# A layer norm inside a convolution module: from tokens on partitions to channels on partitions

## The chip, the cores and the metric

The kernel runs on one core of one Trainium2 chip. The time is device microseconds of one execution. A second source is the profile: one execution recorded instruction by instruction, with its own span, from the first to the last instruction. All positions in microseconds below are counted from the start of that span.

The core has five engines that work side by side, each through its own queue in program order: TensorE (in the profile PE for matrix products and PEld for the loading of their stationary operand), VectorE (DVE), ScalarE (ACT), GpSimd (POOL) and SyncE (SP), which here issues the loads from memory. They wait for each other through semaphores. Operands lie in SBUF, 128 partitions wide; TensorE writes its results into PSUM, and VectorE and ScalarE read and write both.

## The reference

A trunk of two layers over 256 tokens with 2048 channels. Layer 0 mixes tokens with a convolution module, layer 1 with latent attention, and a squared-ReLU MLP follows each. The change lies wholly in the convolution module:

```python
def layer_norm(x, g, b):
    xf = x.astype(jnp.float32)
    mu = jnp.mean(xf, axis=-1, keepdims=True)
    xc = xf - mu
    var = jnp.mean(xc * xc, axis=-1, keepdims=True)
    y = xc * lax.rsqrt(var + LN_EPS) * g.astype(jnp.float32) + b.astype(jnp.float32)
    return y.astype(x.dtype)

def conv_module(h, w_pw1, b_pw1, w_dw, b_dw, ln_g, ln_b, w_pw2, b_pw2):
    u = h @ w_pw1 + b_pw1
    a, gate = jnp.split(u, 2, axis=-1)
    u = a * jax.nn.sigmoid(gate)
    u = lax.conv_general_dilated(
        u, w_dw[:, None, :].astype(u.dtype), window_strides=(1,),
        padding=[(CONV_WIDTH - 1, 0)],
        dimension_numbers=("NWC", "WIO", "NWC"),
        feature_group_count=D_MODEL) + b_dw
    u = jax.nn.silu(layer_norm(u, ln_g, ln_b))
    return u @ w_pw2 + b_pw2
```

The mean and the variance of a token run over all its 2048 channels, so the norm cannot begin before the depthwise convolution of the last channels is done; gain and bias belong to a channel.

## The kernel before

**Data.** The 256 tokens are two blocks of 128 (T = 2), the 2048 channels sixteen chunks of 128 (KC = 16). Every full-precision product is made of three products of fp32r parts: an operand is split into a rounded high part and the rest, and high×high, low×high and high×low are added up in PSUM (`mm3`, L184 to L186). ScalarE makes the high part by a copy (`hi`, L158) and VectorE the rest by a subtraction (`lo`, L159); a unit of weights is split in two halves, by `conv_half`. Weights come through three buffers `raw`, one load of 1 MB to a unit, issued by SyncE; the halves lie in six buffers `hi` and six `lo`. So a load waits until both halves of the unit three before it are split, and a split waits until TensorE is done with the halves three units before.

**The convolution loop** (L712) runs over the chunks c. For each it makes the first pointwise product of the chunk (`conv_mm`), the gated value, and the 31 taps of the depthwise convolution, most of them on VectorE (`dve_tap`, L591). Here channels lie on partitions. The result of a chunk is written to `ca`, a pair of chunks to a tile, two such tiles in turn. Three chunks later TensorE turns it (`to_tokens`, L629), so that tokens lie on partitions and a pair of chunks fills one PSUM tile `ct`; VectorE takes the statistics of the pair from there (`bn_stats`, L639), and ScalarE copies the pair to `cn` (L641), in which all 2048 channels of a token end up on its partition.

**Between the loop and the second product.** TensorE makes transposes of the identity whose result nobody reads (`keep_warm`, counts in `N_WARM_LN`) so as not to stand idle. VectorE joins the statistics (`bn_aggr`, L755), and the function `rsqrt` makes the scale of each token out of the variance, with one square root on ScalarE (L207) and a Newton step on VectorE (L208 to L212). Mean and scale are one number to a token, that is one number to a partition of `cn`.

**The second product** (loop over m, L798) takes two chunks of channels and one 1 MB unit of weights (`NU + m`) to a step, 24 matmuls of 128x512 in all: two chunks by two column blocks by two token blocks by three. Its left operand has channels on partitions again. So `ln_norm` takes mean and scale from `cn` (L766, one VectorE instruction for two chunks of one token block, both factors as scalars of the partition), and `ln_swish` turns the pair back on TensorE (L776, four transposes into a tile `tr`, of which there are two), applies the sigmoid-weighted unit with gain and bias as scalars of the partition (L781, ScalarE), and splits the result into `sh` (L787, ScalarE) and `sl_` (L788, VectorE). The pairs 0 and 1 are done ahead of the loop; in step m stand `ln_norm(m+3)` and `ln_swish(m+2)` ahead of the products, then, in step 0, the second half of weight unit `NU+1`, after its first chunk; then the split of unit `NU+m+2`, the load of unit `NU+m+5`, and one addition of the output bias `b2` to the residual `xs` (L817). After the loop the four sums are added to `xs`, and `product_A` makes the other half of the columns.

Of the kernel before, what the change touches and what calls it, by code (L numbers as in the profile page):

```python
# [18 lines left out]
P = 128  # L19
# [30 lines left out]
LAST_REST = (20, 17, 0)  # L50
FILL_AT = (5, 15)
N_WARM = 14
N_WARM_LN = (8, 26, 14)
EPS = 1e-6
LN_EPS = 1e-5
SCALE = (DN + DR) ** -0.5
# [20 lines left out]
def trunk_kernel(  # L77
# [35 lines left out]
    def repool(name, **banks):  # L113

        psum_cx[0].close()
        psum_cx[0] = ExitStack()
        for kind, n in banks.items():
            psum[kind] = psum_cx[0].enter_context(tc.tile_pool(name=kind + name, bufs=n, space=PSUM, reuse_waits="tile"))
# [13 lines left out]
    def nm(s):  # L132
        uid[0] += 1
        return f"{s}_{uid[0]}"
# [5 lines left out]
    def tr_tile():  # L140
        return psum["tr"].tile([P, NB], F32, tag="tr", name=nm("tr"))
# [295 lines left out]
    with ExitStack() as cx:  # L437
# [10 lines left out]
        xn = cv.tile([P, T, D], F32, tag="tok", name="xn")  # L448
        b2 = cv.tile([P, D], F32, name="b2")

        cn = cv.tile([P, T, D], F32, tag="tok", name="cn")
        sh = cv.tile([P, KC, S], F32R, name="sh")
        sl_ = cv.tile([P, KC, S], F32R, name="sl_")
        stats = cv.tile([P, T, KC // 2, 6], F32, name="stats")
# [35 lines left out]
                    nc.tensor.matmul(o, wh[:, bs], xl(k), start=False, stop=False)  # L490
                    nc.tensor.matmul(o, wl[:, bs], xh(k), start=False, stop=k == KC - 1)  # L491

        pss, ubs, pcs, cas, cts, sides, left = {}, {}, {}, {}, {}, {}, {}
        rest = lambda c: LAST_REST[c - KC + 3] if c > KC - 4 else REST[min(c, 2)]
        n_side = lambda c: LAST_SIDE[c - KC + 3] if c > KC - 4 else SIDE
        tap = lambda c, w: w_dw[:, w * KC + c : w * KC + c + 1]

        def sum_tile():
            return psum["sum"].tile([P, NB], F32, tag="sum", name=nm("sum"))

        def ca_part(c):
            if c // 2 not in cas:
                cas[c // 2] = cv2.tile([P, 2 * S], F32, tag="ca", name=nm("ca"))
            return cas[c // 2][:, c % 2 * S : (c % 2 + 1) * S]

        def glu(c):
            ub = ubs[c] = cv2.tile([P, PAD + S], F32, tag="ub", name=nm("ub"), bufs=3)
# [62 lines left out]
        def dve_tap(c):  # L570
            w = left[c].pop(0)
            out = pcs[c]
            if w is None:
                nc.vector.tensor_tensor(out, out, sides[c][0], op=ALU.add)
                return
            if c == KC - 1 and w == LAST_PE + n_side(c):
                nc.vector.tensor_scalar(
                    out, ubs[c][:, w : w + S], scalar1=tap(c, w), scalar2=b_dw[:, c : c + 1],
                    op0=ALU.mult, op1=ALU.add,
                )  # L580
                return
            if not left[c]:
                if c == KC - 1:
                    half = cv2.tile([P, S], F32, tag="half", name=nm("half"), bufs=1)
                    nc.vector.scalar_tensor_tensor(
                        out=half, in0=ubs[c][:, w : w + S], scalar=tap(c, w), in1=out, op0=ALU.mult, op1=ALU.add
                    )
                    nc.vector.tensor_tensor(ca_part(c), last_sum[0], half, op=ALU.add)
                    return
                out = ca_part(c)  # L590
            nc.vector.scalar_tensor_tensor(  # L591
                out=out, in0=ubs[c][:, w : w + S], scalar=tap(c, w), in1=pcs[c], op0=ALU.mult, op1=ALU.add
            )
# [28 lines left out]
        def to_tokens(c):  # L622

            if c % 2 == 0:
                cts[c // 2] = acc_tile() if c == KC - 2 else tr_tile()
            ct = cts[c // 2]
            for t in range(T):
                q = 2 * t + c % 2
                nc.tensor.transpose(  # L629
                    ct[:, q * P : (q + 1) * P], ca_part(c)[:, t * P : (t + 1) * P], ident  # L630
                )

        def ln_stats(c):
            fill = []
            if c % 2 == 1:
                ct = cts[c // 2]
                for t in range(T):
                    fill.append(
                        lambda t=t: nc.vector.bn_stats(stats[:, t, c // 2, :], ct[:, t * S : (t + 1) * S])  # L639
                    )  # L640
                fill.append(lambda: nc.scalar.activation(  # L641
                    cn[:, :, (c - 1) * P : (c + 1) * P], ct.rearrange("p (t n) -> p t n", t=T), AF.Copy
                ))
            return fill

        conv_load(0)
        conv_load(1)
# [8 lines left out]
        with tc.manual_schedule():  # L656
# [55 lines left out]
            for c in range(1, KC + 1):  # L712
                n = UC * c
                conv_load(n + 3)
                glu(c - 1)
                fill = ln_stats(c - 4 if c < KC else KC - 3) if c > 3 else []
                fill, copies = fill[:T], fill[T:]
                if c < KC:
                    pss[c] = [acc_tile() for _ in range(2)]
                conv_half(n + (c < KC), 0)  # L720
                start_sum(c - 1)
                if c < KC:
                    conv_half(n + 1, 1)
                    dve_taps(c - 1, fill)
                    conv_load(n + 4)
                    side_sum(c - 1)
                    conv_mm(c, 0, 8)
                    if c < KC - 1:
                        conv_half(n + 2, 0)
                        conv_half(n + 2, 1)  # L730
                else:
                    side_sum(c - 1)
                    conv_half(n, 1)
                    conv_half(n + 1, 0)
                    dve_taps(c - 1, fill)
                    conv_load(n + 4)
                for f in copies:
                    f()
                if c < KC:
                    conv_mm(c, 8)  # L740
                    if c > KC - 4:
                        dgs.extend(diag(KC - 1, w) for w in range(len(dgs), min(len(dgs) + 8, LAST_PE)))
                    if c > 2:
                        to_tokens(c - 3)
                    conv_mm(c, 12)
# [7 lines left out]
            mv = small.tile([P, T, 2], F32, tag="mv", name=nm("mv"))  # L753
            for t in range(T):
                nc.vector.bn_aggr(mv[:, t, :], stats[:, t, :, :].rearrange("p a b -> p (a b)"))  # L755
            rl = rsqrt(mv[:, :, 1], T, LN_EPS, "n")
            warm(AF.Silu)
            repool("m", acc=6, tr=2)
            ps2 = [[acc_tile() for _ in range(T)] for _ in range(2)]

            def ln_norm(jj):
                ks = slice(2 * jj * P, (2 * jj + 2) * P)
                for t in range(T):
                    nc.vector.tensor_scalar(  # L766
                        cn[:, t, ks], cn[:, t, ks], scalar1=mv[:, t, 0:1], scalar2=rl[:, t : t + 1],
                        op0=ALU.subtract, op1=ALU.mult,
                    )

            def ln_swish(jj):
                pt = tr_tile()
                for j in range(2):
                    k = 2 * jj + j
                    for t in range(T):
                        nc.tensor.transpose(  # L776
                            pt[:, j * S + t * P : j * S + (t + 1) * P], cn[:, t, k * P : (k + 1) * P], ident
                        )
                for j in range(2):
                    k = 2 * jj + j  # L780
                    nc.scalar.activation(  # L781
                        pt[:, j * S : (j + 1) * S], pt[:, j * S : (j + 1) * S], AF.Silu,
                        bias=ln_b[:, k : k + 1], scale=ln_g[:, k : k + 1],
                    )
                sp = pt.rearrange("p (j n) -> p j n", j=2)
                ks = slice(2 * jj, 2 * jj + 2)
                nc.scalar.activation(sh[:, ks, :], sp, AF.Copy)  # L787
                nc.vector.tensor_tensor(sl_[:, ks, :], sp, sh[:, ks, :].bitcast(F32), op=ALU.subtract)  # L788

            sh_kt = lambda k, t: sh[:, k, t * P : (t + 1) * P]  # L790
            sl_kt = lambda k, t: sl_[:, k, t * P : (t + 1) * P]
            NP = KC // 2
            for jj in range(3):
                ln_norm(jj)
            for jj in range(2):
                ln_swish(jj)
            keep_warm(ident, N_WARM_LN[2])
            for m in range(NP):  # L798
                if m + 3 < NP:
                    ln_norm(m + 3)  # L800
                if m + 2 < NP:
                    ln_swish(m + 2)
                for j in range(2):
                    k = 2 * m + j
                    wh, wl = conv_w(NU + m, j)
                    for b in range(2):
                        bs = slice(b * NB, (b + 1) * NB)
                        for t in range(T):
                            mm3(ps2[b][t], sh_kt(k, t), sl_kt(k, t), wh[:, bs], wl[:, bs], k == 0, k == KC - 1)
                    if m == 0 and j == 0:  # L810
                        conv_half(NU + 1, 1)
                conv_split(NU + m + 2)
                conv_load(NU + m + 5)

                t, i = divmod(m, NNB)
                sl = slice(i * NB, (i + 1) * NB)
                nc.vector.tensor_tensor(xs[:, t, sl], xs[:, t, sl], b2[:, sl], op=ALU.add)  # L817

        ssq, add, prepare = residual_stage(True, g_mlp[0])
        for b in range(2):  # L820
# [590 lines left out]
```

## Time and profile before

| what | us |
|---|---|
| median of three executions | 2000.11 |
| lowest and highest of them | 1999.77 and 2000.18 |
| the profiled execution, its own time | 1998.02 |
| span of that execution, first to last instruction | 1996.2 |
| convolution loop and taps, by position | about 32 to 217 |
| norm until the first of the second products | 217 to 224.2 |
| second product, first half of its columns | 224.2 to 270.2 |

Lines of three views are quoted below. A line of the timeline gives start, duration, engine, line of the kernel, operation, output and inputs, shape, and how many instructions were merged into it; in square brackets stand the idle time before it and what ended that. Merged instructions overlap, so the duration of a line of several is less than the sum of its parts. A line of the groups gives line, engine, operation, shapes and count, then the busy time in us and the mean duration of one in ns, then the idle time before them. A line of the windows gives, for one stretch, the busy time of PE, PEld, DVE, ACT and POOL with the number of instructions, then the granted TensorE clock (1.00 is full), the share of the DMA engines and GB/s.

### The profile page before, as it was taken

How to read it: one execution, taken by the hardware profiler on the slowest of the kernel's cores; microseconds unless marked ns; L12 is line 12 of the kernel's file. 1: busy time of each engine (PE TensorE's matmuls, PEld its weight loads, DVE VectorE, ACT ScalarE, POOL GpSimd, SP SyncE). 2: the span in 40 equal slices, each digit the busy share in tenths (PEclk: the TensorE clock that was granted, in tenths of full speed). 3: DMA queues.
4: the chain of work that ended last, by engine and by line, in shares of the span. 5: the costliest groups of instructions: out<-in, count | busy, mean ns of one | idle time of the engine just before them, and what ended most of it. 6: DMA issues, size and time to landing. Idle time of an engine off the chain costs nothing.

```text
span 1996.2 us, 27870 instructions
## 1 busy us (share of the span) xinstructions
PE 1971.5 (99%) x11060; PEld 1727.9 (87%) x11060; DVE 1214.7 (61%) x1805; ACT 975.7 (49%) x1385; POOL 224.0 (11%) x184
## 2 busy tenths in 40 slices
PE   7999999999999999999999999999999999999998
PEld 7999788888888888888899998888888888888886
DVE  6999867556544555655556665656654545665553
ACT  5456655445333444544456665545443334454443
POOL 5999200000000000000001310000000000000000
PEclk9999999999999999999999999999999999999999
DMA  7666365665555666555555445666655566665653
GB/s 239 185 183 183 130 198 182 190 190 189 195 198 195 190 190 190 190 190 190 190 159 176 120 147 181 200 190 190 190 190 190 195 194 189 191 191 195 194 190 105
DMA packets 243265, 367.57 MB, mean 184 GB/s; under 512 B 15416, under 2 KB 89792, under 8 KB 242880
## 3 DMA queue, kind: packets, MB, share of 16 engines
q1 hardware_dynamic: 242400, 364.68, 57.6%
q8 instruction: 86, 1.41, 0.3%
q10 hardware_dynamic: 736, 1.12, 0.2%
q14 instruction: 43, 0.35, 0.0%
HBM read 363.68 MB, written 2.10 MB: 183 GB/s over the span
## 4 chain that ended last, share of the span: by engine, by line
PE 90%; DVE 8%; ACT 1%; DMA 0%; issue 0%; POOL 0%; SPq 0%; ACTq 0%; DVEq 0%
PE acc L403 23%; PE acc L186 16%; PE acc L184 16%; PE acc L185 16%; PE acc L404 12%; DVE sum L591 6%; PE acc L490 1%; PE acc L489 1%; PE acc L491 1%; PE tr L241 1%; PE sum L539 0%; DMA xs<-in_x 0%; PE acc L1185 0%; ACT hi L158 0%; PE acc L1049 0%
## 5 line engine op out<-in xcount | busy, mean ns | idle before, releaser
L159 DVE TENSOR_TENSOR lo<-raw,hi 128x1024 fp32r<-128x1024 f32 (+2 forms) x630 | 760.9, 1211 | 693.4 <-ACT hi L158 681.6
L158 ACT ACTIVATE hi<-raw 128x1024 fp32r<-128x1024 f32 (+1 forms) x696 | 723.2, 1046 | 787.8 <-PE acc L185 452.2
L403 PE MATMUL acc<-xt,hi 128*128 128x512 f32 x2048 | 710.6, 390 | 0.0
L404 PE MATMUL acc<-xt,lo 128*128 128x256 f32 x2048 | 577.7, 282 | 0.0
L403 PEld LDWEIGHTS acc<-xt,hi 128*128 128x128 f32 x2048 | 384.5, 188 | 80.5
L184 PE MATMUL acc<-hi,gh 128*128 128x512 f32 x1024 | 398.6, 389 | 0.0
L186 PE MATMUL acc<-lo,gh 128*128 128x512 f32 x1024 | 398.4, 389 | 0.0
L185 PE MATMUL acc<-hi,gl 128*128 128x512 f32 x1024 | 398.4, 389 | 0.0
L404 PEld LDWEIGHTS acc<-xt,lo 128*128 128x128 f32 x2048 | 387.1, 189 | 0.1
L185 PEld LDWEIGHTS acc<-hi,gl 128*128 128x128 f32 x1024 | 192.2, 188 | 39.8
L184 PEld LDWEIGHTS acc<-hi,gh 128*128 128x128 f32 x1024 | 192.2, 188 | 39.8
L186 PEld LDWEIGHTS acc<-lo,gh 128*128 128x128 f32 x1024 | 192.2, 188 | 39.8
L591 DVE SCALAR_TENSOR_TENSOR sum<-ub,w_dw,sum 128x256 f32<-128x256 f32 x400 | 162.9, 484 | 7.5 <-ACT sum L547 6.4
L159 POOL TENSOR_TENSOR lo<-raw,hi 128x1024 fp32r<-128x1024 f32 x66 | 157.7, 2413 | 21.7 <-ACT hi L158 21.7
L489 PE MATMUL acc<-xt,hi 128*128 128x256 f32 x512 | 144.4, 282 | 0.0
L490 PE MATMUL acc<-xt,hi 128*128 128x256 f32 x512 | 143.1, 279 | 0.9 <-DVE xt L197 0.9
L491 PE MATMUL acc<-xt,lo 128*128 128x256 f32 x512 | 143.1, 279 | 0.3 <-POOL lo L159 0.3
L490 PEld LDWEIGHTS acc<-xt,hi 128*128 128x128 f32 x512 | 96.3, 188 | 1.1 <-DVE xt L197 1.1
L491 PEld LDWEIGHTS acc<-xt,lo 128*128 128x128 f32 x512 | 96.2, 188 | 0.6 <-POOL lo L159 0.6
L489 PEld LDWEIGHTS acc<-xt,hi 128*128 128x128 f32 x512 | 96.3, 188 | 0.0
L980 POOL MEMSET pad_kv<- 128x8 f32 x1 | 0.1, 105 | 770.1 <-PE acc L186 770.1
L411 ACT ACTIVATE v<-acc 128x256 f32<-128x256 f32 x128 | 46.4, 381 | 25.4 <-PE acc L404 25.4
(240 smaller groups left out, 1785.0 us busy)
## 6 DMA issues: line engine op xcount, KB each, us to landing
raw<-in_mlp_w SPq DMA_DIRECT2D x256, 1024.0 KB, 5.1
raw<-in_conv_w_pw SPq DMA_DIRECT2D x64, 512.0 KB, 5.2
raw<-in_conv_w_pw SPq DMA_DIRECT2D x16, 1024.0 KB, 5.0
raw<-in_mla_w_o SPq DMA_DIRECT2D x16, 1024.0 KB, 5.5
raw<-in_mla_w_kv_up SPq DMA_DIRECT2D x8, 1024.0 KB, 5.5
raw<-in_mla_w_in SPq DMA_DIRECT2D x8, 576.0 KB, 3.7
raw<-in_mla_w_in SPq DMA_DIRECT2D x4, 1024.0 KB, 6.1
raw<-in_mla_w_q_up SPq DMA_DIRECT2D x16, 256.0 KB, 3.8
```

Of the source, the lines that this page charges most:

```text
L158: nc.scalar.activation(hi, raw[:, js, :], AF.Copy)
L159: eng.tensor_tensor(lo, raw[:, js, :], hi.bitcast(F32), op=ALU.subtract)
L184: nc.tensor.matmul(ps, sh, mh, start=start, stop=False)
L185: nc.tensor.matmul(ps, sl, mh, start=False, stop=False)
L186: nc.tensor.matmul(ps, sh, ml, start=False, stop=stop)
L403: nc.tensor.matmul(ps[b], wh[:, bs], xhl(k), start=k == 0, stop=False)
L404: nc.tensor.matmul(ps[b][:, :S], wl[:, bs], xh(k), start=False, stop=k == KC - 1)
L411: nc.scalar.activation(v[:, b, :], o[:, S:], AF.Copy)
L489: nc.tensor.matmul(o, wh[:, bs], xh(k), start=k == 0, stop=False)
L490: nc.tensor.matmul(o, wh[:, bs], xl(k), start=False, stop=False)
L491: nc.tensor.matmul(o, wl[:, bs], xh(k), start=False, stop=k == KC - 1)
L591: nc.vector.scalar_tensor_tensor(out=out, in0=ubs[c][:, w : w + S], scalar=tap(c, w), in1=pcs[c], op0=ALU.mult, op1=ALU.add)
```

## The change

The norm is done where the convolution leaves its result, with channels on partitions. The sixteen chunks are kept in one tile `ca`, which takes the place of `cn`; the copies to `cn` fall away. The transposes of `to_tokens` stay, for the statistics alone. Mean and scale now differ along the row and not along the partitions, so each is spread by two transposes of a column read 128 times over: every partition of the PSUM tiles `mean` and `scale` then holds the 256 values of all tokens. Norming is two VectorE instructions (subtract the row, multiply by the row) in place of one with two scalars; the four transposes of each pair in `ln_swish` fall away, and ScalarE and VectorE work in place on `ca` in SBUF. The first two chunks are done one by one. The additions of `b2` move from all steps to the last three. The counts of idle transposes change.

```diff
-N_WARM_LN = (8, 26, 14)
+N_WARM_LN = (8, 17, 6, 10)
...
-        cn = cv.tile([P, T, D], F32, tag="tok", name="cn")
+        ca = cv.tile([P, KC, S], F32, tag="tok", name="ca")
...
-            fill = []
-            if c % 2 == 1:
-                ct = cts[c // 2]
-                for t in range(T):
-                    fill.append(
-                        lambda t=t: nc.vector.bn_stats(stats[:, t, c // 2, :], ct[:, t * S : (t + 1) * S])
-                    )
-                fill.append(lambda: nc.scalar.activation(
-                    cn[:, :, (c - 1) * P : (c + 1) * P], ct.rearrange("p (t n) -> p t n", t=T), AF.Copy
-                ))
-            return fill
+            if c % 2 == 0:
+                return []
+            ct = cts[c // 2]
+            return [
+                lambda t=t: nc.vector.bn_stats(stats[:, t, c // 2, :], ct[:, t * S : (t + 1) * S])
+                for t in range(T)
+            ]
...
+            repool("m", acc=6, tr=2)
+
+            mean, scale = (tr_tile()[:, :S] for _ in range(2))
+
+            def spread(dst, src):
+                for t in range(T):
+                    nc.tensor.transpose(dst[:, t * P : (t + 1) * P], src(t).broadcast_to([P, P]), ident)
+
+            spread(mean, lambda t: mv[:, t, 0:1])
             rl = rsqrt(mv[:, :, 1], T, LN_EPS, "n")
             warm(AF.Silu)
-            repool("m", acc=6, tr=2)
+            keep_warm(ident, N_WARM_LN[2])
+            spread(scale, lambda t: rl[:, t : t + 1])
             ps2 = [[acc_tile() for _ in range(T)] for _ in range(2)]
...
-            def ln_norm(jj):
-                ks = slice(2 * jj * P, (2 * jj + 2) * P)
-                for t in range(T):
-                    nc.vector.tensor_scalar(
-                        cn[:, t, ks], cn[:, t, ks], scalar1=mv[:, t, 0:1], scalar2=rl[:, t : t + 1],
-                        op0=ALU.subtract, op1=ALU.mult,
+            def ln_op(k, n, row, op):
+                o = ca[:, k : k + n, :]
+                row = row.rearrange("p (a n) -> p a n", a=1).broadcast_to([P, n, S])
+                nc.vector.tensor_tensor(o, o, row, op=op)
+
+            def ln_norm(k, n=2):
+                ln_op(k, n, mean, ALU.subtract)
+                ln_op(k, n, scale, ALU.mult)
+
+            def ln_swish(k, n=2):
+                for j in range(k, k + n):
+                    nc.scalar.activation(
+                        ca[:, j, :], ca[:, j, :], AF.Silu, bias=ln_b[:, j : j + 1], scale=ln_g[:, j : j + 1]
                     )
...
+                nc.scalar.activation(sh[:, k : k + n, :], ca[:, k : k + n, :], AF.Copy)
+                nc.vector.tensor_tensor(
+                    sl_[:, k : k + n, :], ca[:, k : k + n, :], sh[:, k : k + n, :].bitcast(F32), op=ALU.subtract
+                )
...
-            for jj in range(3):
-                ln_norm(jj)
-            for jj in range(2):
-                ln_swish(jj)
-            keep_warm(ident, N_WARM_LN[2])
+
+            for row, op in ((mean, ALU.subtract), (scale, ALU.mult)):
+                for k in range(2):
+                    ln_op(k, 1, row, op)
+            for k in range(2):
+                ln_swish(k, 1)
+            ln_norm(2)
+            ln_swish(2)
+            ln_norm(4)
+            keep_warm(ident, N_WARM_LN[3])
             for m in range(NP):
                 if m + 3 < NP:
-                    ln_norm(m + 3)
+                    ln_norm(2 * (m + 3))
                 if m + 2 < NP:
-                    ln_swish(m + 2)
+                    ln_swish(2 * (m + 2))
...
-                t, i = divmod(m, NNB)
-                sl = slice(i * NB, (i + 1) * NB)
-                nc.vector.tensor_tensor(xs[:, t, sl], xs[:, t, sl], b2[:, sl], op=ALU.add)
+                for q in {NP - 3: (0, 1, 4), NP - 2: (5, 2, 3), NP - 1: (6, 7)}.get(m, ()):
+                    t, i = divmod(q, NNB)
+                    sl = slice(i * NB, (i + 1) * NB)
+                    nc.vector.tensor_tensor(xs[:, t, sl], xs[:, t, sl], b2[:, sl], op=ALU.add)
```

More of the change, by code (lines that the diff above doesn't have):

```diff
@@ L491, in conv_mm @@
                     nc.tensor.matmul(o, wl[:, bs], xh(k), start=False, stop=k == KC - 1)
-        pss, ubs, pcs, cas, cts, sides, left = {}, {}, {}, {}, {}, {}, {}
+        pss, ubs, pcs, cts, sides, left = {}, {}, {}, {}, {}, {}
         rest = lambda c: LAST_REST[c - KC + 3] if c > KC - 4 else REST[min(c, 2)]
@@ L499, in sum_tile @@
             return psum["sum"].tile([P, NB], F32, tag="sum", name=nm("sum"))
[L501 to L504, printed above, removed]
         def glu(c):
@@ L587, in dve_tap @@
                     )
-                    nc.vector.tensor_tensor(ca_part(c), last_sum[0], half, op=ALU.add)
+                    nc.vector.tensor_tensor(ca[:, c, :], last_sum[0], half, op=ALU.add)
                     return
-                out = ca_part(c)
+                out = ca[:, c, :]
             nc.vector.scalar_tensor_tensor(
@@ L629, in to_tokens @@
                 nc.tensor.transpose(
-                    ct[:, q * P : (q + 1) * P], ca_part(c)[:, t * P : (t + 1) * P], ident
+                    ct[:, q * P : (q + 1) * P], ca[:, c, t * P : (t + 1) * P], ident
                 )
         def ln_stats(c):
-            fill = []
-            if c % 2 == 1:
-                ct = cts[c // 2]
-                for t in range(T):
-                    fill.append(
-                        lambda t=t: nc.vector.bn_stats(stats[:, t, c // 2, :], ct[:, t * S : (t + 1) * S])
-                    )
-                fill.append(lambda: nc.scalar.activation(
-                    cn[:, :, (c - 1) * P : (c + 1) * P], ct.rearrange("p (t n) -> p t n", t=T), AF.Copy
-                ))
-            return fill
+            if c % 2 == 0:
[5 more added lines that the diff above has]
+            ]
         conv_load(0)
@@ L716, in trunk_kernel @@
                 fill = ln_stats(c - 4 if c < KC else KC - 3) if c > 3 else []
-                fill, copies = fill[:T], fill[T:]
                 if c < KC:
@@ L736, in trunk_kernel @@
                     conv_load(n + 4)
-                for f in copies:
-                    f()
                 if c < KC:
@@ L759, in trunk_kernel @@
+            spread(scale, lambda t: rl[:, t : t + 1])
             ps2 = [[acc_tile() for _ in range(T)] for _ in range(2)]
-            def ln_norm(jj):
-                ks = slice(2 * jj * P, (2 * jj + 2) * P)
-                for t in range(T):
-                    nc.vector.tensor_scalar(
-                        cn[:, t, ks], cn[:, t, ks], scalar1=mv[:, t, 0:1], scalar2=rl[:, t : t + 1],
-                        op0=ALU.subtract, op1=ALU.mult,
-                    )
[L771 to L788, printed above, removed]
```

## The prediction

> **What bounds the kernel now.** First the page: the busy shares, and the engines of the chain that ended last.
>
> ```profile
> PE 1971.5 (99%) x11060; PEld 1727.9 (87%) x11060; DVE 1214.7 (61%) x1805; ACT 975.7 (49%) x1385; POOL 224.0 (11%) x184
> ...
> PE 90%; DVE 8%; ACT 1%; DMA 0%; issue 0%; POOL 0%; SPq 0%; ACTq 0%; DVEq 0%
> ```
>
> TensorE sets the end nearly everywhere; VectorE's 8% lie in the convolution taps and in the norm. So the change can gain where TensorE waits for the norm, and where TensorE itself is relieved. Then the windows of the stages that it touches.
>
> ```profile
> 100.00:140.00 40.00, 40.00 (x345) 40.00 (x344) 40.00 (x104) 24.12 (x38) 38.36 (x26) 1.00 0.64 189
> ...
> 203.50:206.90 3.40, 1.34 (x8) 1.03 (x7) 3.40 (x11) 2.51 (x5) 2.42 (x3) 1.00 0.49 200
> 217.00:220.40 3.40, 3.01 (x29) 2.77 (x26) 2.76 (x12) 2.29 (x4) 0.00 (x0) 1.00 0.00 0
> 220.40:224.20 3.80, 3.42 (x27) 2.80 (x27) 2.21 (x6) 2.80 (x6) 0.00 (x0) 1.00 0.00 0
> ```
>
> In the loop PE and DVE are full and ACT is busy 24 of 40 us. From 217 to 224.2 PE looks busy, but with idle transposes. Last, the timeline of that stretch and of the product behind it, all engines.
>
> ```profile
> 216.97 3.00 PE L224 MATMUL acc<-ident 128*128 128x128 f32 x26
> ...
> 217.84 0.58 DVE L755 BATCH_NORM_AGGREGATE mv<-stats 128x2 f32<-128x48 f32 x2
> ...
> 219.70 0.16 DVE L212 TENSOR_TENSOR y<-y,t 128x2 f32<-128x2 f32 x1
> 219.89 2.03 DVE L766 TENSOR_SCALAR cn<-cn,mv,y 128x256 f32<-128x256 f32 x6
> ...
> 221.27 1.11 ACT L781 ACTIVATE tr<-tr,vecs 128x256 f32<-128x256 f32 x2 [0.89 <-PE tr L776]
> ...
> 223.04 0.69 DVE L788 TENSOR_TENSOR sl__119<-tr,sh 128x512 fp32r<-128x512 f32 x1 [1.12 <-ACT sh L787]
> 223.79 0.42 PEld L776 LDWEIGHTS tr<-ident,cn 128*128 128x128 f32 x4 [0.62 <-DVE sl__119 L788]
> ...
> 224.20 0.48 PE L184 MATMUL acc<-hi,sh 128*128 128x512 f32 x1
> ...
> 224.51 0.39 PE L185 MATMUL acc<-hi,sl__119 128*128 128x512 f32 x1
> ...
> 226.16 2.95 ACT L158 ACTIVATE hi<-raw 128x1024 fp32r<-128x1024 f32 x3
> ...
> 227.25 3.50 DVE L159 TENSOR_TENSOR lo<-raw,hi 128x1024 fp32r<-128x1024 f32 x3 [0.25 <-ACT hi L158]
> ...
> 254.35 0.40 PE L186 MATMUL acc<-lo,sh 128*128 128x512 f32 x1
> ...
> 270.24 0.39 PE L184 MATMUL acc<-hi,sh 128*128 128x512 f32 x1
> ```
>
> The scale is ready at 219.86 (219.70 + 0.16). From there the chain runs through norm, turn, ScalarE, VectorE and, because two `tr` tiles hold three pairs, once more through a turn; the first product starts at 224.20, the second at 224.51. The loop has 192 matmuls; the third of step 5 starts at 254.35 and 70 further on, at 270.24, `product_A` begins: 15.89 / 70 = 0.227 a matmul. From the second product, 191 matmuls would be 43.36; they took 270.24 - 224.51 = 45.73, so the five groups of four transposes in the loop cost 2.37.
>
> **The change, part by part.** The prices, from the groups of the whole span with shapes kept apart, ScalarE and then VectorE:
>
> ```profile
> L158 ACT ACTIVATE hi<-raw 128x1024 fp32r<-128x1024 f32 x672 | 707.4, 1060 | 771.2 <-PE acc L185 435.7 <-PE acc L403 301.7 <-ACT gh L415 26.2
> ...
> L415 ACT ACTIVATE gh<-v 128x512 fp32r<-128x512 f32 x64 | 40.5, 633 | 6.1 <-DVE v L413 6.1
> ...
> L547 ACT ACTIVATE sum<-ub,vecs,w_dw 128x256 f32<-128x256 f32 x15 | 8.5, 570 | 0.8 <-POOL ub L520 0.8
> ...
> L511 ACT ACTIVATE sg<-acc,vecs 128x256 f32<-128x256 f32 x16 | 7.6, 475 | 78.1 <-PE acc L491 78.1
> ...
> L641 ACT ACTIVATE cn<-tr 128x512 f32<-128x512 f32 x7 | 4.0, 578 | 3.3 <-DVE stats L639 3.3
> L190 ACT ACTIVATE qhl<-qp 128x256 fp32r<-128x256 f32 x8 | 3.5, 433 | 1.2 <-POOL qp L899 1.2
> ```
> ```profile
> L159 DVE TENSOR_TENSOR lo<-raw,hi 128x1024 fp32r<-128x1024 f32 x606 | 742.6, 1228 | 675.0 <-ACT hi L158 663.3 <-PE tr L241 9.6
> ...
> L416 DVE TENSOR_TENSOR gl<-v,gh 128x512 fp32r<-128x512 f32 x64 | 43.8, 685 | 0.0
> ...
> L325 DVE TENSOR_TENSOR xs<-acc,xs 128x512 f32<-128x512 f32 x16 | 10.6, 688 | 3.0 <-PE acc L186 3.0
> ...
> L817 DVE TENSOR_TENSOR xs<-xs,b 128x512 f32<-128x512 f32 x8 | 5.3, 684 | 0.0
> ...
> L588 DVE TENSOR_TENSOR ca<-sum,half 128x256 f32<-128x256 f32 x1 | 0.4, 425 | 0.1
> ```
>
> *Copies to `cn`*, eight of about 0.58: nothing. ScalarE has 16 of 40 us free in the loop while PE and DVE are full; without that cover they would be 4.6. The end of the taps, on VectorE, does not move, so 219.86 stays.
>
> *Mean row*: `bn_aggr` ends at 218.42, the two transposes follow the 17 idle ones (216.97 + 17 x 3.00/26 = 218.9) and are done before 219.8, when VectorE comes free of the Newton step: hidden. Were they late, they would delay the chain one for one.
>
> *Scale row*: on the path. Two transposes after 219.86; VectorE has it at about 220.45. Meanwhile it subtracts chunks 0 and 1 (row L588, starting every 0.33), so the wait for the row costs little.
>
> *First products.* Operations that follow each other start 0.03 to 0.06 after the one they wait for, as in the timeline (L788 and the turn behind it). Multiply 0 at 220.45 to 220.88 (L588). The sigmoid unit out of SBUF does not occur before; between L511 (0.475, one scalar of the partition, from PSUM) and L547 (0.570, two, from SBUF) I take 0.57 to 0.58, as it has two scalars and reads SBUF: to 221.50. High part (L190, 0.43) to 221.95, rest to 222.40. First product 222.0, second 222.46 in place of 224.51: 2.05 earlier. The idle transposes, 6 and 10, end by about 221.5, ahead of it.
>
> *Turns gone from the loop*: 2.37. Together 4.42, if nothing else ends later.
>
> *What is queued behind.* The order of ScalarE and VectorE puts the second half of weight unit `NU+1` behind the swish of the pairs 1 and 2, as before; but before, the norms of three pairs stood first and ran in 2.03. Now VectorE does: rest of chunk 1 (222.92), subtract 2-3 (223.25 to 223.94), multiply (223.98 to 224.67), then waits for ScalarE: two units starting 0.49 apart and a high part (L415) to 226.43; rest (L416) 226.46 to 227.15; subtract 4-5 from 227.06, multiply to 228.48 (L325 twice); ScalarE again to 230.24, and only then the weights: `hi` 230.15 to 231.21, `lo` 231.24 to 232.47 (L158, L159). Before, this `lo` started at 227.25 and ended 1.2 later. TensorE wants it for the third matmul of chunk 3, the 39th: 222.46 + 37 x 0.227 = 230.86. It gets it at 232.53. So 1.67 of the 4.42 go back into a wait that was not there, half for `hi`, half for `lo`. From there 154 matmuls end at 232.53 + 34.96 = 267.49 in place of 270.24.
>
> Chunks 4 and 5 find their weights (`lo` at 233.6 and 234.8, wanted from 235.2 and 237.9). Later steps need of VectorE two of 0.69, one of 0.69 and two of 1.23, 4.5 against 5.45 of products, with norms a step ahead: no wait.
>
> *Loads*: SyncE issues in the same order; the buffer of unit `NU+1` comes free 4 later, at 232.5.
>
> ```profile
> raw<-in_conv_w_pw SPq DMA_DIRECT2D x14, 1024.0 KB, 5.0
> ```
>
> Landing at 237.5, unit `NU+4` is wanted for step 4 at about 245.7, after 1.06 and 1.23 of splitting: 6 to spare. *Additions of `b2`*: eight of L817, 5 us of VectorE within the last three steps (16 us); if late they would hold the additions of the sums after 267.5.
>
> Sum, on the profiled execution: 2.05 + 2.37 - 1.67 = 2.75, span 1996.2 to 1993.45. Its own time was 1998.02, 2.09 below the median shown; the difference is taken over to the median: 2000.11 - 2.75 = 1997.4. Bounds: with L511's price in every unit the chain up to `lo` is 0.6 shorter, gain 3.3; with 0.1 in place of 0.04 at each of some ten handovers it is 0.6 longer, gain 2.1. The forecast's own range is 1996.8 to 1998.0.
>
> [...]
>
> **Rivals.** *The weights arrive in time* (0.29). If the chain from the scale to that `lo` is 1.7 of some 12 shorter, the whole 4.42 stays: 1995.7. For it: the reads leave PSUM, and the idle gaps of VectorE there are waits for ScalarE alone. Against: it needs more than the best price in the rows gives.
>
> *The gain is given back behind the loop* (0.06): if `b2` or the splits for `product_A` come late, up to 2.75 is lost: 1997.4 to 2000.1. Against: VectorE was busy 61%, and PE was never held there by it.
>
> *Rows read over and over are slow* (0.06). Every subtraction and multiplication reads a PSUM row twice in one instruction, which no row shows. If that makes each 0.69 longer by e, the chain up to `lo`, with four of them and three halves, is 5.5 e longer: the gain is gone at e = 0.5, and at e = 1.24 the kernel is 4 slower, 2004. Against: L325 reads PSUM at the price of L817, which does not.
>
> *The clock falls* (0.03). From the last taps to the first product TensorE has transposes alone, now fewer of them and with about 1.2 us of waits. At half clock each us of products costs another; 8.4 (37 matmuls) would turn 4.42 into 4 slower. Against: the windows show 1.00 through 217 to 224.2, and at 203.5 with 1.34 busy of 3.40. [...]
>
> **How the numbers follow.** Forecast 0.56, and the rivals as given. 0.2% is 4.0, about what can be told from no change here. Faster is the case of weights in time, 0.29; same is the forecast and the giving back, 0.62; slower are the last two, 0.09. The range reaches from below 1995.7, with 0.4 for error, to 1999.3, which takes in most of the giving back.
>
> **What would show it.** No L776; two transposes each for mean and scale; the second product at 222.5 (if at 223 or later, the prices of ScalarE or the rows are wrong); a wait of PE for `hi` and `lo` before the third matmul of chunk 3 at 230 to 232.5, 1.7 in all (none: the first rival); subtract and multiply at 0.69; steps of 5.45 from step 2 on; `product_A` at 267.5; clock 1.00. A stall in any later step, or a start of `product_A` that does not come through to the end, would make it wrong.

## The result, and the profile after

The changed kernel takes 1996.95 us (median of 20 executions, 1995.12 to 1997.19), beside 1999.63 for the one before in the same comparison (20 executions, 1997.96 to 2000.18). The ratio is 0.9987, with a 95% interval from 0.9981 to 0.9993: shorter by 0.13%, which is less than the 0.2% that the prediction took for the least that can be told from no change. The forecast was 1997.4. Two executions of the versions tried further below, of 3915 and 2985 us where all others lie between 1993 and 2001, are left out of every count.

First the page of the changed kernel: busy shares, and the engines of the chain that ended last.

```profile
span 1995.1 us, 27788 instructions
...
PE 1970.5 (99%) x11025; PEld 1726.1 (87%) x11025; DVE 1219.0 (61%) x1808; ACT 972.5 (49%) x1378; POOL 223.9 (11%) x184
...
PE 89%; DVE 8%; ACT 1%; DMA 0%; issue 0%; POOL 0%; SPq 0%; ACTq 0%; DVEq 0%
```

The span is 1995.1 in place of 1996.2, so 1.1 shorter, where the median moved by 2.7. The two profiled executions do not tell the same story as the medians, and the timeline of TensorE says why. Of the changed kernel:

```profile
205.69 6.70 PE L534 MATMUL sum<-ub,dg 128*128 128x256 f32 x22 [2.02 <-DVE ub L509]
212.23 0.38 PE L624 MATMUL tr<-ident,ca 128*128 128x128 f32 x2
212.45 4.92 PE L534 MATMUL sum<-ub,dg 128*128 128x256 f32 x22
```

And of the kernel before, the same instructions under their old line number:

```profile
205.83 5.02 PE L539 MATMUL sum<-ub,dg 128*128 128x256 f32 x22 [2.06 <-DVE ub L514]
```

These are the taps of the last chunk that TensorE takes over. The change does not touch them, nor the pause of 2.0 ahead of them, yet the first 22 take 6.70 and not 5.02. The windows of the changed kernel, whose number behind the POOL column is the granted clock, show the reason:

```profile
203.50:205.60 2.10, 0.16 (x2) 0.00 (x0) 2.10 (x8) 1.42 (x2) 1.12 (x3) 1.00 0.77 314
205.60:207.00 1.40, 1.31 (x4) 1.16 (x5) 1.40 (x5) 1.33 (x4) 1.40 (x1) 0.72 0.04 12
207.00:208.50 1.50, 1.50 (x5) 1.16 (x4) 1.50 (x5) 1.50 (x3) 1.50 (x3) 0.50 0.00 0
208.50:210.00 1.50, 1.50 (x6) 1.20 (x5) 1.50 (x5) 1.48 (x2) 1.42 (x3) 0.62 0.00 0
```

In this execution the clock fell to half just behind the pause, 0.5 into the taps: a mean of 0.72 over 1.40 puts the fall at 206.2, and 0.62 over the last 1.50 puts the return at 209.6. In the profiled execution of before it was 1.00 in the window over the pause, and the taps behind it took 5.02. Everything behind lies later by what was lost, 1.68 less the 0.14 by which the taps began earlier. So positions are compared from the scale on: it is ready at 221.40 here (L212, below) and was at 219.86, a shift of 1.54. The timelines of VectorE, ScalarE and TensorE in that stretch of the changed kernel:

```profile
221.24 0.16 DVE L212 TENSOR_TENSOR y<-y,t 128x2 f32<-128x2 f32 x1
221.32 1.41 DVE L763 TENSOR_TENSOR ca<-ca,tr 128x256 f32<-128x256 f32 x4
223.51 0.42 DVE L775 TENSOR_TENSOR sl__119<-ca,sh 128x256 fp32r<-128x256 f32 x1 [0.78 <-ACT sh L774]
...
228.03 0.69 DVE L775 TENSOR_TENSOR sl__119<-ca,sh 128x512 fp32r<-128x512 f32 x1 [1.83 <-ACT sh L774]
228.63 2.72 DVE L763 TENSOR_TENSOR ca<-ca,tr 128x512 f32<-128x512 f32 x4
...
232.81 3.50 DVE L159 TENSOR_TENSOR lo<-raw,hi 128x1024 fp32r<-128x1024 f32 x3 [0.25 <-ACT hi L158]
```
```profile
222.43 0.60 ACT L771 ACTIVATE ca<-ca,vecs 128x256 f32<-128x256 f32 x1 [0.50 <-DVE ca L763]
...
226.23 1.10 ACT L771 ACTIVATE ca<-ca,vecs 128x256 f32<-128x256 f32 x2 [1.81 <-DVE ca L763]
...
230.07 1.09 ACT L771 ACTIVATE ca<-ca,vecs 128x256 f32<-128x256 f32 x2 [2.08 <-DVE ca L763]
231.19 0.63 ACT L774 ACTIVATE sh<-ca 128x512 fp32r<-128x512 f32 x1
231.73 2.94 ACT L158 ACTIVATE hi<-raw 128x1024 fp32r<-128x1024 f32 x3
```
```profile
223.53 0.50 PE L184 MATMUL acc<-hi,sh 128*128 128x512 f32 x1 [0.55 <-ACT sh L774]
223.99 0.50 PE L185 MATMUL acc<-hi,sl__119 128*128 128x512 f32 x1
...
232.83 0.50 PE L184 MATMUL acc<-hi,sh 128*128 128x512 f32 x1 [0.60 <-ACT hi L158]
233.16 0.40 PE L185 MATMUL acc<-hi,sl__119 128*128 128x512 f32 x1
234.09 0.50 PE L186 MATMUL acc<-lo,sh 128*128 128x512 f32 x1 [0.53 <-DVE lo L159]
...
269.15 0.39 PE L184 MATMUL acc<-hi,sh 128*128 128x512 f32 x1
```

What these lines show is a relay. VectorE waits 1.83 for ScalarE (at 228.03), ScalarE 2.08 for VectorE (at 230.07), and only behind both stand the weights, `hi` at 231.73 and `lo` at 232.81. Taken back by 1.54, the second product starts at 222.45 (forecast 222.46), that `lo` at 231.27 (231.24), the third matmul of chunk 3 at 232.55 (232.53) and `product_A` at 267.61 (267.49). The two idle times of TensorE, 0.60 and 0.53, are less than the delay of 1.70 that the starts give (234.09 - 223.99 less 37 x 0.227), because the profile counts a matmul as busy for 0.39 to 0.50 where in a full stretch the next one starts after 0.227. No turn stands between the products any more.

### The profile page after: what moved, and what is told of

Its sections match the earlier page's. It is cut to its first block, busy times and chain, and to the rows that moved or that the text cites. A ratio compares the mean times of both kernels' runs of the same rounds, so it can differ in the third digit from the quotient of the medians.

```text
span 1995.1 us, 27788 instructions
## 1 busy us (share of the span) xinstructions
PE 1970.5 (99%) x11025; PEld 1726.1 (87%) x11025; DVE 1219.0 (61%) x1808; ACT 972.5 (49%) x1378; POOL 223.9 (11%) x184
## 4 chain that ended last, share of the span: by engine, by line
PE 89%; DVE 8%; ACT 1%; DMA 0%; issue 0%; POOL 0%; SPq 0%; ACTq 0%; DVEq 0%
PE acc L403 23%; PE acc L184 16%; PE acc L186 16%; PE acc L185 16%; PE acc L404 12%; DVE sum L586 6%; PE acc L490 1%; PE acc L489 1%; PE acc L491 1%; PE tr L241 1%; PE sum L534 1%; DMA xs<-in_x 0%; ACT hi L158 0%; DVE lo L159 0%; PE acc L1180 0%
```

## Experiments

Each experiment was run beside the kernel before. From one set of runs to the next the kernel before varies in the share of executions that lie near 1999.8 and not near 1998.1 (12 of 20 in the first comparison; 8 of 30, 12 of 31 and 6 of 12 in the later sets, the first and the last of these on one chip), so the single times say more than the median. In the first comparison they were:

```
before:   8 from 1997.96 to 1998.17, 12 from 1999.60 to 2000.18
changed:  5 from 1995.12 to 1995.62, 15 from 1996.78 to 1997.19
```

Two levels in each kernel, about 1.6 to 1.7 apart, as much as the taps lost in the profile (6.70 - 5.02 = 1.68). By the medians of the levels the change is worth 1998.06 - 1995.39 = 2.67 on the lower and 1999.79 - 1996.98 = 2.81 on the upper.

**The late weights.** Edit, on the changed kernel:

```diff
             ln_norm(2)
+            conv_half(NU + 1, 1)
             ln_swish(2)
...
-                    if m == 0 and j == 0:
-                        conv_half(NU + 1, 1)
```

> The split of the second half of weight unit NU+1 moves ahead of the swish of chunks 2 and 3, into a stretch where ScalarE and VectorE wait for each other. Theory (that half is late, and TensorE waits for it before chunk 3): the wait before the third matmul of chunk 3 is gone and no later one takes its place, 1.5 to 1.7 us less than the changed kernel, median near 1995.3. Rival (the wait only moves: the rest of chunks 2 and 3, or of chunk 4, comes late instead): less than 0.5 us, and a wait in chunk 2 or 4.

Measured: 1995.28, ratio to before 0.9979 (0.997 to 0.9988). Seven times lie from 1995.25 to 1995.45 and three from 1993.59 to 1993.78: both levels, each about 1.7 below the changed kernel's. The time of the wait comes back in full. That it does not move to another place is read from the profile of the run with both edits, below.

**The pause ahead of the taps.** Edit, on the changed kernel: sixteen idle transposes, queued on TensorE in front of the taps.

```diff
                 last_sum.append(o)
+                keep_warm(ident, 16)
```

> Sixteen idle transposes fill the 2 us in which TensorE waits for the gated values of the last chunk, ahead of the last taps. Theory (the two levels of the times, 1.6 us apart in both kernels, come from a clock that falls to half in that gap in some executions and not in others): only the lower level is left, all runs at 1995.1 to 1995.7, and the taps show a clock of 1.00. Rival (the levels come from somewhere else, the start or the loads): both levels stay, median near 1997.

Measured: 1995.36; ten times from 1995.13 to 1995.87. The upper level is gone. TensorE in the profile of this run:

```profile
203.67 1.91 PE L224 MATMUL acc<-ident 128*128 128x128 f32 x16
205.85 5.02 PE L534 MATMUL sum<-ub,dg 128*128 128x256 f32 x22 [0.27 <-DVE ub L509]
...
222.01 0.50 PE L184 MATMUL acc<-hi,sh 128*128 128x512 f32 x1 [0.56 <-ACT sh L775]
222.47 0.50 PE L185 MATMUL acc<-hi,sl__119 128*128 128x512 f32 x1
...
231.32 0.50 PE L184 MATMUL acc<-hi,sh 128*128 128x512 f32 x1 [0.60 <-ACT hi L158]
232.58 0.50 PE L186 MATMUL acc<-lo,sh 128*128 128x512 f32 x1 [0.53 <-DVE lo L159]
```

The pause is 0.27, the taps take 5.02 again, and the clock in the windows from 203.5 to 217 is 1.00. This trace can be laid beside that of before as it stands: second product at 222.47 against 224.51, waits for `hi` and `lo` of 0.60 and 0.53 at the forecast place. The cause of the two levels in the changed kernel is thereby shown: this version and the four below that have the gap filled and otherwise keep TensorE supplied (both edits, and the three that put something back) have 48 executions, and none of the five shows a second level.

**Both edits.**

> The two edits together. Theory: they add up, one level at 1993.6 to 1994.0, 5.5 to 6 us below the median of before. Rival (the late weights were covered by the slow taps, or the reverse): no better than the better of the two alone, 1995.2.

Measured: 1993.72, all eight times from 1993.56 to 1994.20, ratio 0.9974 (0.9964 to 0.9985). They add up, and this version beats both kernels: 4.3 below the lower level of before. It is 4.5 and not 5.5 to 6 below the median of before, because that median was 1998.23 here, on the lower level. Its VectorE and TensorE:

```profile
223.42 1.40 DVE L764 TENSOR_TENSOR ca<-ca,tr 128x512 f32<-128x512 f32 x2
224.74 1.22 DVE L159 TENSOR_TENSOR lo<-raw,hi 128x1024 fp32r<-128x1024 f32 x1
226.65 0.69 DVE L776 TENSOR_TENSOR sl__119<-ca,sh 128x512 fp32r<-128x512 f32 x1 [0.69 <-ACT sh L775]
227.26 2.72 DVE L764 TENSOR_TENSOR ca<-ca,tr 128x512 f32<-128x512 f32 x4
```
```profile
224.20:270.00 45.80, 45.80 (x204) 37.94 (x203) 41.78 (x51) 33.05 (x48) 0.00 (x0) 1.00 0.61 207
```

The subtraction of the weights takes up 1.2 of VectorE's wait for ScalarE, 0.69 in place of 1.83, and delays nothing: TensorE is busy all 45.80 of the window (second fence).

**The pause in the kernel before.** The same line added to the kernel before.

> The kernel of before with the same sixteen idle transposes in the same gap. Theory (the clock there has nothing to do with the change): one level at 1998.0 to 1998.2, so that the change is worth 2.5 to 2.8 us level against level. Rival (the clock falls more often because of the change, and before mostly keeps it): no shift of the median beyond 0.3 us.

Measured: 1998.16, ratio 0.9997 (0.9989 to 1.0006). The median did not move, as the rival has it, but in this set before itself was mostly on the lower level (22 of 30 runs below 1998.8), so the median cannot decide. Of the eleven times eight lie from 1998.04 to 1998.48; 1998.72, 1999.14 and 1999.71 are left. The spans, from the first to the last instruction, decide. All eleven are from 1996.0 to 1996.5, those of the three late ones 1996.1, so what holds these three up lies outside the instructions. In the 73 executions of before in the three later sets, 26 spans are from 1997.6 to 1998.1 and 47 from 1995.9 to 1996.7. So the upper level is gone here too, though eleven executions are few. Against this median, the changed kernel with the gap filled is 2.80 faster (1998.16 - 1995.36).

**Turns in the loop.** Edit, on the version with the gap filled, with a PSUM tile `idle` of its own (the ten idle transposes ahead of the loop write to it as well):

```diff
                     ln_swish(2 * (m + 2))
+                    if m > 0:
+                        idle_turns(4)
```

> On the changed kernel with the gap filled (1995.4): four idle transposes, which wait for nothing, put ahead of the products of steps 1 to 5, where the kernel of before had its turns. Theory (each group costs TensorE 0.47 us, but the group of step 1 lies in front of the late weights and is hidden by that wait): 4 x 0.47 = 1.9 us more, 1997.2. Rivals: all five count, 2.4 us more; or the transposes slip between the products and cost little, below 1 us.

Measured: 1997.15, ten times from 1997.05 to 1997.28: 1.79 above the version with the gap filled. Two of the five groups in TensorE's timeline:

```profile
227.81 0.60 PE L796 MATMUL acc<-ident 128*128 128x128 f32 x4
...
232.52 0.50 PE L186 MATMUL acc<-lo,sh 128*128 128x512 f32 x1 [0.53 <-DVE lo L159]
...
234.95 0.60 PE L796 MATMUL acc<-ident 128*128 128x128 f32 x4
```

And of VectorE, the first addition of the sums behind the loop:

```profile
267.62 0.69 DVE L325 TENSOR_TENSOR xs<-acc,xs 128x512 f32<-128x512 f32 x1 [1.31 <-PE acc L186]
```

The first group stands ahead of the late weights: the third matmul of chunk 3 starts at 232.52, not later than without it. The other four cost 1.79 / 4 = 0.45 each by the times. By the traces it is 0.47: the first addition of the sums stands at 267.62, and at 265.79 with the gap filled alone (below), where the first product started 0.05 later, so 1.88 / 4. Five groups in a loop without a wait are thus worth 2.2 to 2.4.

**Fewer idle transposes.** On the version with both edits:

```diff
-N_WARM_LN = (8, 17, 6, 10)
+N_WARM_LN = (8, 1, 1, 1)
```

> On the version with the gap filled and the weights early (1993.7): one idle transpose in place of 17, of 6 and of 10 in the norm, so that TensorE stands still for some 4 of the 6 us between the last taps and the first product. Theory (idle transposes keep the clock up as matmuls do, and without them it falls as it did in the 2 us gap): half clock at the first products and 1.5 to 2 us more in most runs, near 1995.4. Rival (transposes do not count as work for the clock, so that they were of no use): no change, 1993.7.

Measured: 1995.15, ten times spread from 1994.71 to 1996.60, so 1.0 to 2.9 above the version with both edits, 1.4 by the medians, where 1.5 to 2 was expected. Windows and TensorE's timeline of its profile, the shortest of the ten:

```profile
218.50:222.00 3.50, 0.97 (x7) 0.49 (x6) 2.31 (x11) 2.81 (x6) 0.00 (x0) 0.91 0.00 0
222.00:225.50 3.50, 3.50 (x10) 2.72 (x11) 2.95 (x5) 2.60 (x5) 0.00 (x0) 0.60 0.00 0
225.50:229.00 3.50, 3.50 (x17) 2.91 (x16) 2.77 (x5) 1.39 (x3) 0.00 (x0) 1.00 0.60 161
```
```profile
221.95 0.80 PE L184 MATMUL acc<-hi,sh 128*128 128x512 f32 x1 [1.53 <-ACT sh L775]
222.54 0.66 PE L185 MATMUL acc<-hi,sl__119 128*128 128x512 f32 x1
223.00 0.63 PE L186 MATMUL acc<-lo,sh 128*128 128x512 f32 x1
223.43 0.63 PE L184 MATMUL acc<-hi,sh 128*128 128x512 f32 x1
```

With TensorE busy 0.97 of 3.50 the clock fell, to a mean of 0.91 in that window and of 0.60 in the next, and from the second on the first products start 0.42 to 0.46 apart in place of 0.227. So the idle transposes kept the clock up here, and the 33 of the changed kernel were enough: its clock from 217.3 to 223.5 is 1.00.

**The copies, and the additions of `b2`, put back** (each alone, on the version with the gap filled): ScalarE copies every pair from PSUM to a spare tile as before; and

```diff
-                for q in {NP - 3: (0, 1, 4), NP - 2: (5, 2, 3), NP - 1: (6, 7)}.get(m, ()):
+                for q in (m,):
```

> On the changed kernel with the gap filled (1995.4): ScalarE copies each pair out of PSUM again, at the places of before, to a tile that nobody reads. Theory (ScalarE has time to spare in the loop of the convolution, and the copies never lay on the path): no change, within 0.2 us. Rival (they held back what follows on ScalarE, the gated values above all): 0.5 us or more.

> On the changed kernel with the gap filled (1995.4): the additions of the output bias back to one in each step. Theory (VectorE has about 1 us of each step to spare, also with the longer norm): no change, within 0.2 us. Rival (an addition in the first steps makes the splits of the weights late once more): 0.5 us or more, with a wait of TensorE in steps 1 to 3.

Measured: 1995.41 with the copies (1995.32 to 1996.06) and 1995.57 with the additions (1995.48 to 1995.75), beside 1995.36. The copies cost nothing that can be told. The additions lie 0.2 above 1995.36, which was taken in another set, and 0.16 above the copies, which were run in the same one; whether they cost that, or where, is not shown. In their trace the only waits of TensorE after the first product are the two for the late weights, and the first addition of the sums starts where it does in the version with the gap filled. First fence: additions in the steps; second: the gap filled alone.

```profile
265.79 0.69 DVE L325 TENSOR_TENSOR xs<-acc,xs 128x512 f32<-128x512 f32 x1 [1.31 <-PE acc L186]
```
```profile
265.79 0.69 DVE L325 TENSOR_TENSOR xs<-acc,xs 128x512 f32<-128x512 f32 x1 [1.31 <-PE acc L186]
```

**The first two chunks as a pair.** On the version with both edits:

```diff
-            for row, op in ((mean, ALU.subtract), (scale, ALU.mult)):
-                for k in range(2):
-                    ln_op(k, 1, row, op)
-            for k in range(2):
-                ln_swish(k, 1)
+            ln_norm(0)
+            ln_swish(0)
```

> On the version with the gap filled and the weights early (1993.7): chunks 0 and 1 as one pair, like all others, and not one by one. Theory (the chain from the scale to the first products sets the end, and 256 columns pass through it faster than 512): subtract and multiply 0.69 each, two sigmoid units and a high part of 512, so that the second product starts 1.3 us later, 1995.0. Rival (the start of the first products is not what counts, since later steps have waits that take it up): below 0.3 us.

Measured: 1996.07, five times from 1995.05 to 1995.34 and five from 1996.81 to 1997.21. The profile is of one of the former:

```profile
223.08 0.50 PE L184 MATMUL acc<-hi,sh 128*128 128x512 f32 x1 [1.65 <-ACT sh L775]
223.80 0.50 PE L185 MATMUL acc<-hi,sl__119 128*128 128x512 f32 x1 [0.22 <-DVE sl__119 L776]
```

The lower group, with a middle of 1995.2, lies 1.5 above the version with both edits; 1.3 was expected. The start of the first products sets the end. The upper group is another 1.9 higher, about as much as a fall of the clock cost before (1.68); the pause ahead of the first product is 1.65 here, where it was 0.55. That the clock falls in this pause in every second execution fits, but it is not shown: there is no profile of such an execution, and in this one the clock stayed at 1.00.

## Why the prediction was right

*Start of the products* (2.05 us forecast): 222.47 in the version with the gap filled against 224.51 before, 2.04. The prices held. The sigmoid unit out of SBUF takes 0.59 to 0.60 (L771, sixteen at a mean of 0.592), with 0.57 to 0.58 taken. Subtract and multiply with a row read over take what L588 and L325 gave. The group of the changed kernel:

```profile
L763 DVE TENSOR_TENSOR ca<-ca,tr 128x512 f32<-128x512 f32 x14 | 9.5, 683 | 0.2
```

The price was 0.688. So the rival of the slow rows falls.

*Turns* (2.37): 0.45 to 0.47 for each group by the experiment, 2.2 to 2.4 for five.

*The wait for the weights* (1.67): 234.09 against 223.99 + 37 x 0.227 = 232.39, so 1.70, and 1.6 to 1.7 came back when that half was split early. This was the term that decided between 1995.7 and 1997.4, and the rival in which the weights are in time falls with it.

*Nothing behind the loop*: the 154 matmuls behind the wait take 269.15 - 234.09 = 35.06, with 34.96 reckoned. Between the two profiles in which the clock stayed at 1.00 over the pause and the taps, before and the gap filled, the first addition of the sums (L325) moves from 268.40 to 265.79, 2.61, and the span is 2.5 shorter (1996.2 to 1993.7): what is gained is still there at the end.

*The copies and the additions at nothing*: borne out for the copies, for the additions to within 0.2.

Two steps of the prediction did not hold, though the sum does not show it. The time of the profiled execution was carried over to the median as if the 2.09 between them were a constant. Most of it was the distance of the two levels, 1.73 by their medians. The sum came out right by luck, because the medians of both kernels lay on the upper level in this comparison. Had the changed kernel's stood on its lower one, near 1995.4, the same mechanism would have missed the forecast's own range; and in two of the later sets the median of before was 1998.2.

The other step is the rival of the clock. It was put behind the last taps, and dismissed with the window from 203.5, 1.34 busy of 3.40 at clock 1.00. That was one execution: in others the clock falls at just that pause, in the changed kernel's profile and, by the run with that pause filled, in before as well. The place was wrong, and one trace with a clock of 1.00 does not show that a pause is safe. How that execution differed from the changed kernel's is told in the last section.

## What to carry to other kernels

When a chain on two engines is cut short so that a third can start earlier, look at what stood behind the chain in their queues: here the split of the next weights kept its place in the order and became late as its consumer came early, which took 1.7 of 4.4; the remedy was a slot where both engines wait for each other anyway. Reckon the gain from the point where the chain branches off and price each link from a row of the same shape and memory; the links came out to within 0.1 in sum. And before a profile is compared with a profile, look at the spread of the times: with two levels a pair of profiles can be off by their distance. Here the two spans differed by 1.1, and the change is worth 2.7.

## What the runs showed of the hardware

With a pause of 2.0 in TensorE's work ahead of the taps (2.02 in the changed kernel, 2.06 in before) the clock fell to 0.50 in the profiled execution of the changed kernel and stayed at 1.00 in that of before. By the levels, which makes it an estimate, it fell in 15 of 20 executions of the changed kernel and 12 of 20 of before in one comparison, and in 8 of 30 of before in another. The loss of 1.68 in the taps at a clock of 0.50 means that it lasted about 3.4, and the windows gave 206.2 to 209.6.

In these two executions the pause lies differently among steps of 3.413 us. In the trace of the changed kernel the recorded clock is full from 15.07, half from 206.22 to 209.63, full to 1991.39 and half at the end; the three stretches in between, 191.15, 3.41 and 1781.76, are 56, 1 and 522 times 3.41333. In that of before it is full from 13.64 to 1989.96, 579 times 3.41333 (1976.32), and half at the end. Counted on in such steps, edges lie there at 201.37, 204.78 and 208.20, the middle one within the pause. Each window below is one step, first of the changed kernel, then of before:

```profile
202.81:206.22 3.41, 1.39 (x10) 1.14 (x9) 3.41 (x11) 1.97 (x4) 2.43 (x4) 1.00 0.66 269
206.22:209.63 3.41, 3.41 (x9) 2.69 (x8) 3.41 (x10) 3.39 (x6) 3.33 (x4) 0.50 0.02 5
...
1984.56:1987.98 3.42, 1.79 (x8) 1.14 (x7) 0.75 (x1) 0.72 (x2) 0.00 (x0) 1.00 0.24 83
1987.98:1991.39 3.41, 0.00 (x0) 0.00 (x0) 2.06 (x7) 1.54 (x3) 0.00 (x0) 1.00 0.22 83
1991.39:1994.80 3.41, 0.00 (x0) 0.00 (x0) 0.00 (x0) 0.00 (x0) 0.00 (x0) 0.50 0.65 224
```
```profile
201.37:204.78 3.41, 2.40 (x21) 2.20 (x19) 3.41 (x10) 0.92 (x2) 3.01 (x5) 1.00 0.83 267
204.78:208.20 3.42, 2.37 (x11) 2.10 (x12) 3.42 (x11) 2.90 (x6) 2.84 (x2) 1.00 0.12 46
...
1986.54:1989.96 3.42, 0.88 (x4) 0.38 (x3) 1.34 (x4) 0.93 (x3) 0.00 (x0) 1.00 0.01 2
1989.96:1993.37 3.41, 0.00 (x0) 0.00 (x0) 1.46 (x5) 1.33 (x2) 0.00 (x0) 0.50 0.51 187
```

In the changed kernel the whole pause lay in one step, which left TensorE 1.39 busy of 3.41, and the next step ran at half clock. In before the edge cut the pause in two, the steps were busy for 2.40 and 2.37, and full clock followed on both. Counted in this way the two traces hold 1158 steps with a step behind them. Three of these were busy for 1.39 or less, one around the pause and one at the end of each program (0.00 and 0.88), and half clock followed on every one. All others were busy for 1.79 or more, and full clock followed on every one. That is three falls in two executions; what a step between 1.39 and 1.79 would bring they do not show.

Transposes held the full clock in these runs. With sixteen of them in the pause it was 1.00 from 203.5 to 217, and the upper level was gone; with three in place of 33 in the norm it fell to a mean of 0.60 over the first 3.5 us of products. Whether they would also bring it back from half, no run shows.
